# A transformer block in which the token range is worked in two halves from attention on, and a second block of tokens fetches its expert rows

## The chip, the cores and the metric

The kernel runs on one core of one Trainium2 chip. The metric is the device time of one execution in microseconds (us). A core has a matrix engine (PE, with its weight loads listed as PEld), a vector engine (DVE), a scalar engine (ACT), a general engine (POOL) and queues that issue transfers (SP above all). Sixteen DMA engines move data between HBM and the on-chip memory.

## What is computed

One layer on 512 tokens of width 2048, all in float32:

```python
h = rmsnorm(x, norm_mix_g)
proj = einsum('bsd,de->bse', h, w_in)
o_a = mla_branch(...)                  # 8 heads, chunk-causal softmax attention
o_b = dsa_branch(...)                  # 8 heads, keys chosen by a top-256 index score
merged = gate[0] * (o_a @ w_branch_a) + gate[1] * (o_b @ w_branch_b)
x = x + merged @ w_out
x = x + peer_ffn(rmsnorm(x, norm_ffn_g), ...)
return rmsnorm(x, norm_final_g)
...
# peer_ffn, for each token t: 8 heads x 16 experts of 16384 are chosen
a = gelu(einsum('thkd,td->thk', u_emb[expert], xb))
out = einsum('thk,thkd->td', softmax(top_s) * a, v_emb[expert])
```

The 512 tokens are four blocks of 128, called 0 to 3. U and V are the expert tables, 16384 rows of 2048 numbers each (134 MB each).

## The kernel before

**Precision.** Large matrix products are made of three products: each operand is split into a high part `hi` (rounded by ACT, line 77) and a rest `lo` (a subtraction of two on-chip tiles, line 78), and `mm3` (lines 101 to 104) adds hi*hi, hi*lo and lo*hi. `wload` loads 512 KB of weights, and splits them; the subtraction is DVE's unless `eng` names POOL.

**Order of the stages.** `mixing` projects the input and does attention for all four blocks. `emit` then forms the gated branches (loop over `f`, lines 151 to 166; 512 columns a product) and the output projection with the residual (lines 177 to 189; each weight load serves four blocks). `peer` normalises, asks which experts each token chooses (`wq`, then the top-16 searches of lines 684 to 699 on DVE), and evaluates them in two ways:

- Block 0 (`GB`) is fetched: `gathers` (lines 617 to 633) fetches 128 times one U row for each of the 128 tokens with an indirect DMA that POOL issues, and DVE multiplies and sums (line 623); then 128 times one V row, which DVE scales and adds to the sum (line 632). The row buffer `r` has three places.
- Blocks 1 to 3 are dense: `u_chunk` (lines 602 to 613) multiplies 128 experts at a time with 384 tokens, and `g_d`, a table in HBM with the weight of every expert for every token, made by `weights` (lines 734 to 774), switches off all that were not chosen. V is then multiplied in 16 groups of 8 chunks (lines 820 to 875), with 512 columns of V a product and three token blocks as weights.

**What sets the order.** The 54 (`NS`) first U chunks are done before V begins, along with `weights`, and wait in HBM (`s_d`); the other 74 are done group by group beside V. `tick` hands out the 256 fetches of block 0 over the V stage, each tied behind a `mark` instruction. Each engine executes its instructions in a fixed order that the planner wrote out at build time.

Of the kernel before, what the change touches and what calls it, by code (L numbers as in the profile page):

```python
# [30 lines left out]
NEXP = 16384  # L31
ND = 3
TD = ND * P
GB = 0
NS = 54
# [17 lines left out]
def emit(tc, a, out, dbg=None):  # L53
    nc = tc.nc
    with ExitStack() as top:
# [3 lines left out]
        ident = cp.tile([P, P], F32, name="ident")  # L59

        sig_d = dr.tile([KT, P, 2, S], F32, name="sig_d")
        x1_d = dr.tile([NB, P, D], F32, name="x1_d")
        s_d = dr.tile([NS, P, TD], F32, name="s_d")
        g_d = dr.tile([TD // TG, P, P * TG], F32, name="g_d")
        h2_d = dr.tile([P, D], F32, name="h2_d")

        def wload(src, eng=None):

            n = 1
            for d_ in src.shape[1:]:  # L70
                n *= d_
# [8 lines left out]

        def xraw(src):
            raw = wp.tile([P, 1024], F32, name="raw", tag="raw", bufs=4)
            nc.sync.dma_start(raw, src)
            return raw

        def rows_by_cols(pw, src, xh, xl, eng=None, head=0):

            ws = [None] * 8
            order = [(q, tb) for tb in range(NB) for q in range(head)]
            order += [(q, tb) for q in range(head, 5) for tb in range(NB)]  # L90
            order += [(q, tb) for tb in range(NB) for q in range(5, 8)]
            for q, tb in order:
                if ws[q] is None:
                    ws[q] = wload(src[q], eng)
# [37 lines left out]
        p_st, o_st, m_st, mh_st, x1_st, hg_st = [ExitStack() for _ in range(6)]  # L132
        ps = p_st.enter_context(tc.tile_pool(name="ps", bufs=2, space=PSUM))
        with ExitStack() as mix:
            oT = mixing(tc, nc, a, dbg, mix, o_st, ps, ident, sig_d, wload, mm3, rstd_of, xraw)
        if dbg:
            dbg("oT", oT)


        ohl = m_st.enter_context(tc.tile_pool(name="ohl", bufs=1))  # L140
        oh = ohl.tile([P, 16, S], F32R, name="oh")
        ol = ohl.tile([P, 16, S], F32R, name="ol")
        for k in range(16):
            nc.scalar.copy(oh[:, k, :], oT[:, k, :])
            nc.vector.tensor_sub(ol[:, k, :], oT[:, k, :], oh[:, k, :].bitcast(F32))
        o_st.close()
        mhl = mh_st.enter_context(tc.tile_pool(name="mhl", bufs=1, side="right"))
        mh = mhl.tile([P, KT, S], F32R, name="mh")
        ml = mhl.tile([P, KT, S], F32R, name="ml")
        with tc.tile_pool(name="mt", bufs=2) as tp:  # L150
            for f in range(KT):
                sg = tp.tile([P, 2, S], F32, name="sgl")
                nc.sync.dma_start(sg, sig_d[f])
                pa = []
                for br in range(2):
                    wh, wl = wload(a["wbr"][f, br])
                    pm = ps.tile([P, S], F32, name="pm", tag=("mm", "po")[br])
                    for k in range(8):
                        mm3(pm, wh[:, k * P:(k + 1) * P], wl[:, k * P:(k + 1) * P],
                            oh[:, 8 * br + k, :], ol[:, 8 * br + k, :], k == 0, k == 7)  # L160
                    pa.append(pm)
                nc.vector.tensor_mul(sg[:, 0, :], pa[0], sg[:, 0, :])
                nc.vector.tensor_mul(sg[:, 1, :], pa[1], sg[:, 1, :])
                nc.gpsimd.tensor_add(sg[:, 0, :], sg[:, 0, :], sg[:, 1, :])
                nc.scalar.copy(mh[:, f, :], sg[:, 0, :])
                nc.vector.tensor_sub(ml[:, f, :], sg[:, 0, :], mh[:, f, :].bitcast(F32))
        m_st.close()
        hgp = hg_st.enter_context(tc.tile_pool(name="hg", bufs=1))
        hg = [hgp.tile([P, KT, P], F32R, name="hgh"), hgp.tile([P, KT, P], F32R, name="hgl")]
        x1p = x1_st.enter_context(tc.tile_pool(name="x1", bufs=1))  # L170
        xg = x1p.tile([P, NB, D], F32, name="xg")
        ssq = cp.tile([P, NB, 4], F32, name="ssq")
        np_ = x1_st.enter_context(tc.tile_pool(name="n2", bufs=2))
        grow = np_.tile([P, D], F32, name="grow", bufs=1)
        nc.sync.dma_start(grow, a["gffn_row"])
        with tc.tile_pool(name="mt2", bufs=4) as tp:
            for db in range(4):
                pw = [ps.tile([P, 512], F32, name=f"pw{tb}", tag=("sc", "tr", "mm", "po")[tb]) for tb in range(NB)]
                rows_by_cols(pw, a["wo"][db], lambda tb, k: mh[:, k, tb * P:(tb + 1) * P],
                             lambda tb, k: ml[:, k, tb * P:(tb + 1) * P])  # L180
                for tb in range(NB):
                    xs = tp.tile([P, 512], F32, name="xs")
                    nc.sync.dma_start(xs, a["x"][tb * P:(tb + 1) * P, db * 512:(db + 1) * 512])
                    nc.vector.tensor_add(xs, pw[tb], xs)
                    sq = tp.tile([P, 512], F32, name="sqx", bufs=2)
                    nc.scalar.activation(sq, xs, AF.Square, accum_out=ssq[:, tb, db:db + 1])
                    (nc.vector if db == 3 else nc.gpsimd).tensor_mul(
                        xg[:, tb, db * 512:(db + 1) * 512], xs, grow[:, db * 512:(db + 1) * 512])
                    nc.scalar.dma_start(x1_d[tb, :, db * 512:(db + 1) * 512], xs)
        mh_st.close()  # L190
        if dbg:
            dbg("x1", x1_d)
        peer(tc, nc, a, dbg, out, cp, ident, p_st, x1_st, hg_st, xg, hg, np_, ps, grow, ssq, x1_d, s_d, g_d, h2_d, wload, rows_by_cols, mm3, rstd_of, turn_norm)


def mixing(tc, nc, a, dbg, mix, outer, ps, ident, sig_d, wload, mm3, rstd_of, xraw):

    mp = mix.enter_context(tc.tile_pool(name="mix", bufs=1))
    cm = mp.tile([P, 5, P], F32, name="cm")
    R_M, K_1, K_R, I_1, I_R = [cm[:, j, :] for j in range(5)]  # L200
    cmask = mp.tile([P, S], F32, name="cmask")
    ones = mp.tile([P, P], F32, name="ones")
    nc.vector.memset(ones, 1.0)
    gq = mp.tile([P, 6], F32, name="gq")
    cos0 = mp.tile([P, S], F32, name="cos0")
# [24 lines left out]
    def rope_near(dst, src, cs, half, tp):  # L230
# [7 lines left out]
        dst = sh if dst is None else dst  # L238
        nc.vector.tensor_add(dst, t1, sh)
        return dst  # L240

    def stacked(two, lo, src):

        for t in two:
# [734 lines left out]
```

## Time and profile before

| | us |
|---|---|
| median of three runs | 3678.89 (3674.55 to 3680.96) |
| profiled execution | 3671.36 |
| its span, first to last instruction | 3669.3 |

"Busy" is time in which at least one instruction of an engine runs, waits inside the instruction included. Matrix products overlap, so their cost is read from the distance between their starts. [...] MB is a million bytes.

### The profile page before, as it was taken

Reading aid. Unit: us, or ns where it says so; the run is one execution under the profiler, and the core shown is the slowest. Engines: PE = TensorE matmul, PEld = TensorE weight load, DVE = VectorE, ACT = ScalarE, POOL = GpSimd, SP = SyncE. Lnnn points to the kernel's source line nnn. Section 1 sums busy time; section 2 is a strip of 40 time slices with the busy share of each in tenths; the row PEclk is TensorE's granted clock in tenths of the full one; section 3 lists DMA queues with packets and bytes.
Section 4 is the critical chain, followed back from the end, with each engine's and each line's share of the span. In section 5 each row is a group of like instructions: output and inputs, shape, how many; then the busy total and the mean of one; then the engine's idle time right before and its main releaser. Section 6 shows DMA issues by size and latency. Waiting matters only on the chain.

```text
span 3669.3 us, 46374 instructions
## 1 busy us (share of the span) xinstructions
PE 3588.8 (98%) x17863; PEld 3151.9 (86%) x17863; DVE 2477.1 (68%) x3587; ACT 1223.0 (33%) x1621; POOL 818.2 (22%) x522
## 2 busy tenths in 40 slices
PE   8999999999999999889999999999999999999998
PEld 7878888778888789889998877889989988998997
DVE  8687322357432459999725877878777777777775
ACT  5432222245222323345433322323323322332333
POOL 3001000000101142565301222233222222222221
PEclk9999999999999999999999999999999999999999
DMA  5322333310544424445757898888788888888874
GB/s 164 105 83 92 113 120 116 114 41 27 155 149 138 138 75 135 161 148 200 257 153 237 313 316 304 316 306 325 293 309 335 291 309 323 310 299 323 318 285 169
DMA packets 259852, 767.26 MB, mean 209 GB/s; under 512 B 20528, under 2 KB 84912, under 8 KB 222128
## 3 DMA queue, kind: packets, MB, share of 16 engines
q1 hardware_dynamic: 204480, 446.43, 37.5%
q0 software_dynamic: 36864, 268.45, 18.8%
q10 hardware_dynamic: 18288, 49.42, 3.5%
q8 instruction: 140, 2.29, 0.2%
q14 instruction: 80, 0.66, 0.1%
HBM read 708.00 MB, written 53.61 MB: 208 GB/s over the span
## 4 chain that ended last, share of the span: by engine, by line
PE 90%; DVE 6%; DMA 1%; issue 1%; ACT 1%; POOL 0%; SPq 0%; DVEq 0%; ACTq 0%; POOLq 0%
PE pv L103 9%; PE pv L102 9%; PE pv L104 9%; PE pu L104 9%; PE pu L103 9%; PE pu L102 9%; PE pm L102 8%; PE pm L103 8%; PE pm L104 8%; PE pg L757 2%; PE pw L103 2%; PE pw L102 2%; PE pw L104 2%; DVE lo L78 1%; DMA s<-s_d 1%
## 5 line engine op out<-in xcount | busy, mean ns | idle before, releaser
L78 DVE TENSOR_TENSOR lo<-raw,hi 128x1024 fp32r<-128x1024 f32 (+1 forms) x700 | 888.9, 1274 | 803.3 <-issue 290.5
L77 ACT CAST hi<-raw 128x1024 fp32r<-128x1024 f32 (+1 forms) x722 | 758.9, 1052 | 1862.5 <-PE pu L103 553.0
L104 PE MATMUL pu<-h2h,lo 128*128 128x384 f32 x2048 | 698.7, 341 | 1.7 <-DVE lo L78 1.7
L102 PE MATMUL pu<-h2h,hi 128*128 128x384 f32 x2048 | 696.1, 340 | 0.5 <-ACT s L612 0.5
L103 PE MATMUL pu<-h2l,hi 128*128 128x384 f32 x2048 | 695.5, 340 | 0.0
L103 PE MATMUL pv<-lo,ch 128*128 128x512 f32 x1552 | 605.1, 390 | 12.6 <-DVE lo L78 12.6
L104 PE MATMUL pv<-hi,cl 128*128 128x512 f32 x1552 | 601.0, 390 | 0.0
L102 PE MATMUL pv<-hi,ch 128*128 128x512 f32 x1552 | 588.0, 390 | 4.5 <-ACT ch L836 3.1
L621 POOL DMA_INDIRECT r<-in_u,idx x128 | 238.5, 1863 | 767.4 <-DVE dots L623 737.8
L104 PEld LDWEIGHTS pu<-h2h,lo 128*128 128x128 f32 x2048 | 387.3, 189 | 2.9 <-DVE lo L78 2.4
L102 PEld LDWEIGHTS pu<-h2h,hi 128*128 128x128 f32 x2048 | 387.3, 189 | 1.2 <-ACT s L612 0.8
L103 PEld LDWEIGHTS pu<-h2l,hi 128*128 128x128 f32 x2048 | 387.0, 189 | 0.5
L103 PE MATMUL pm<-lT,hi 128*128 128x512 f32 (+1 forms) x912 | 356.4, 391 | 0.0
L102 PE MATMUL pm<-hT,hi 128*128 128x512 f32 (+1 forms) x912 | 356.1, 390 | 0.0
L103 PEld LDWEIGHTS pv<-lo,ch 128*128 128x128 f32 x1552 | 292.1, 188 | 74.1 <-DVE lo L78 13.9
L104 PE MATMUL pm<-hT,lo 128*128 128x512 f32 (+1 forms) x912 | 355.7, 390 | 0.0
L102 PEld LDWEIGHTS pv<-hi,ch 128*128 128x128 f32 x1552 | 292.0, 188 | 66.1 <-ACT ch L836 3.8
L104 PEld LDWEIGHTS pv<-hi,cl 128*128 128x128 f32 x1552 | 292.1, 188 | 60.7
L630 POOL DMA_INDIRECT r<-in_v,idx x128 | 205.5, 1605 | 575.1 <-DVE acc L632 554.3
L632 DVE SCALAR_TENSOR_TENSOR acc<-r,dots,acc 128x2048 f32<-128x2048 f32 x128 | 300.1, 2345 | 0.2
L623 DVE CUSTOM_DVE_ANT_0 r<-r,h2g 128x2048 f32<-128x2048 f32 x128 | 288.7, 2286 | 3.2 <-DMA r<-in_u,idx 3.2
L103 PEld LDWEIGHTS pm<-lT,hi 128*128 128x128 f32 x912 | 171.7, 188 | 39.1 <-issue 3.4
(291 smaller groups left out, 4371.1 us busy)
## 6 DMA issues: line engine op xcount, KB each, us to landing
raw<-in_ut SPq DMA_DIRECT2D x256, 512.0 KB
raw<-in_v SPq DMA_DIRECT2D x256, 512.0 KB
raw<-in_win SPq DMA_DIRECT2D x114, 512.0 KB
g_d<-gs ACTq DMA_DIRECT2D x24, 1024.0 KB
gt<-g_d SPq DMA_DIRECT2D x16, 1536.0 KB
raw<-in_wbr SPq DMA_DIRECT2D x32, 512.0 KB
raw<-in_wo SPq DMA_DIRECT2D x32, 512.0 KB
s_d<-s ACTq DMA_DIRECT2D x54, 192.0 KB
```

The lines of the kernel that those rows point to most:

```text
L77: nc.scalar.copy(hi, raw)
L78: (eng or nc.vector).tensor_sub(lo, raw, hi.bitcast(F32))
L102: nc.tensor.matmul(ps, wh, xh, start=first, stop=False)
L103: nc.tensor.matmul(ps, wh, xl, start=False, stop=False)
L104: nc.tensor.matmul(ps, wl, xh, start=False, stop=last)
L621: nc.gpsimd.indirect_dma_start(out=r, out_offset=None, in_=a["u"], in_offset=bass.IndirectOffsetOnAxis(ap=idx[:, j:j + 1], axis=0))
L623: nc.vector.tensor_tensor_reduce(out=r, in0=r, in1=h2g, scale=1.0, scalar=0.0, op0=ALU.mult, op1=ALU.add, accum_out=dots[:, j:j + 1])
L630: nc.gpsimd.indirect_dma_start(out=r, out_offset=None, in_=a["v"], in_offset=bass.IndirectOffsetOnAxis(ap=idx[:, j:j + 1], axis=0))
L632: nc.vector.scalar_tensor_tensor(accs[GB], r, dots[:, j:j + 1], accs[GB], ALU.mult, ALU.add)
L757: end[0] = nc.tensor.matmul(pg[:, j], o2[:, j, :], og[:, j, :], start=True, stop=True)
```

## The change

From attention on, everything is done for blocks 0 and 1 first and then for blocks 2 and 3.

- `attention`, `branches` and `residual` are called twice, with 256 columns a product where there were 512. Weights are loaded and split twice; keys and values of the first half are computed twice. `other()` gives every second `lo` of these stages to POOL.
- After the first half the experts of blocks 0 and 1 are asked for (`queries`). Their top-16 searches (`experts_of`) run as `side_work`, one head after each attention head of the second half.
- Block 1 fetches its U rows too. Its scores go into `g_d` in place of the softmax weights, so that its V stays dense: U has 256 dense tokens (`TU`) and V 384 (`TD`).
- `Pace` hands out 384 fetches in the order U of block 1, U of block 0, V of block 0, from the second half's `branches` on: 0.2 per us of planned time, 0.06 during the first 24 U chunks, 0.2 after them, and what is left evenly over the V stage. `weights` of block 1 first takes all fetches up to the 128th.
- `NS` is 104, and one step of `weights` is taken per chunk instead of three. `low` gives POOL one of the two `lo` of each of the first 104 chunks, and of every second one of the rest; in the V stage POOL has one `lo` of four. A second copy of V, `vd`, lies in HBM so that a load has 4 KB runs instead of 2 KB.

```diff
-GB = 0
-NS = 54
+TU = 2 * P
+NS = 104
...
+    def tick(self, mark, weight):
+        self.due += weight * self.rate
+        while self.due >= 1.0:
+            self.due -= 1.0
+            self.taken += 1
+            with self.tc.issue_after(mark.ins):
+                next(self.steps, None)
+
+    def upto(self, n):
+        while self.taken < n:
+            self.taken += 1
+            next(self.steps, None)
...
+        def other():
+
+            turn_w[0] += 1
+            return nc.gpsimd if turn_w[0] % 2 else nc.vector
...
+        def gathers():
+
+            for b in (1, 0):
+                for j in range(P):
+                    r = rp.tile([P, D], F32, name="r")
+                    nc.gpsimd.indirect_dma_start(out=r, out_offset=None, in_=a["u"],
+                                                 in_offset=bass.IndirectOffsetOnAxis(ap=idx[b][:, j:j + 1], axis=0))
+                    nc.vector.tensor_tensor_reduce(out=r, in0=r, in1=h2g[b], scale=1.0, scalar=0.0,
+                                                   op0=ALU.mult, op1=ALU.add, accum_out=dots[b][:, j:j + 1])
...
+        RATE = (0.2, 0.06, 0.2)
...
+        def low(c):
+
+            return (nc.gpsimd if c < NS or c % 2 else None, None)
...
+        fetch = Pace(tc, gathers(), RATE[0])
...
+        for i in range(2):
+            blocks = (2 * i, 2 * i + 1)
...
+                attention(i, oT, lambda mark, weight: None, side_work)
...
+                branches(i, mh, ml, oh, ol, tick, side_work)
...
+                residual(i, mh, ml, xg, grow, tick)
...
+                    for half in range(2):
+                        pw = queries(0, half, parts, ps)
...
+                side_work = experts_of(qT, aq)
...
+                    if tb == 1:
+                        fetch.upto(P)
+                        key, g = key1, dots[1]
...
+                def routes():
+                    for tb in (2, 3, 1):
+                        yield from weights(tb - 1, tb)
...
-            for c in range(NS - NF):
-                s = u_chunk(c, (nc.gpsimd if c < 6 else None, None))
-                nc.scalar.dma_start(s_d[c], s)
-                for _ in range(3):
-                    next(todo, None)
+                for c in range(NS - NF):
+                    s, mark = u_chunk(c, low(c))
                     nc.scalar.dma_start(s_d[c], s)
+                    fetch.rate = RATE[1] if c < 24 else RATE[2]
+                    tick(mark, 5.7)
+                    steps += 103.0 / (NS - NF)
+                    while steps >= 1.0:
+                        steps -= 1.0
+                        next(todo, None)
...
+            fetch.rate = (3 * P - fetch.taken) / ((P - NS) * 5.7 + P * 8.2 - 30.0)
...
+                            s3 = s.rearrange("p (b t) -> p b t", t=TG)
+                            nc.vector.tensor_mul(s3, s3, gt[:, P // TG:, ci, :])
+                            parts3 = [(gt[:, :P // TG, ci, :], slice(0, P)), (s3, slice(P, TD))]
+                            for src, w in parts3:
+                                h3, l3 = [t[:, w].rearrange("p (b t) -> p b t", t=TG) for t in (hi, lo)]
+                                nc.scalar.copy(h3, src)
+                                mark = nc.vector.tensor_sub(l3, src, h3.bitcast(F32))
...
+                                ws[q] = wload(a["vd"][c // 2, db], nc.gpsimd if q == 1 else None)
```

## Rows read from the trace of the kernel before

**Rows 1.** Busy time by engine, from the page.

```profile
PE 3588.8 (98%) x17863; PEld 3151.9 (86%) x17863; DVE 2477.1 (68%) x3587; ACT 1223.0 (33%) x1621; POOL 818.2 (22%) x522
```

**Rows 2.** Stretches: us; busy PE, PEld, DVE, ACT, POOL; clock, DMA share, GB/s.

```profile
709.00:900.00 191.00, 185.88 (x1146) 157.71 (x1145) 117.09 (x408) 93.59 (x230) 10.32 (x8) 1.00 0.13 38
900.00:1074.00 174.00, 173.97 (x766) 143.80 (x767) 76.57 (x93) 49.77 (x61) 20.05 (x15) 1.00 0.46 142
1074.00:1254.00 180.00, 180.00 (x775) 144.97 (x773) 56.29 (x68) 45.43 (x65) 19.91 (x15) 1.00 0.43 139
...
1375.00:1967.00 592.00, 564.57 (x3417) 556.45 (x3415) 468.42 (x881) 245.19 (x285) 219.82 (x158) 0.98 0.53 174
1967.00:2380.00 413.00, 399.01 (x1745) 329.33 (x1746) 331.78 (x385) 125.20 (x150) 102.87 (x56) 0.99 0.89 312
2380.00:3593.00 1213.00, 1213.00 (x6133) 1111.80 (x6132) 945.41 (x822) 373.68 (x439) 337.07 (x197) 1.00 0.85 309
```

**Rows 3.** The stretch of the normalisation and of `wq`.

```profile
1254.00:1375.00 121.00, 115.02 (x562) 96.24 (x561) 65.84 (x316) 39.19 (x56) 43.90 (x27) 0.97 0.31 98
```

**Rows 4.** Timeline of PE, U products: start, us, line, tiles, shape.

```profile
1900.11 0.34 PE L102 MATMUL pu<-h2h,hi 128*128 128x384 f32 x1
...
1906.87 0.34 PE L102 MATMUL pu<-h2h,hi 128*128 128x384 f32 x1
```

**Rows 5.** Timeline of PE, products of 272 columns at the start.

```profile
35.82 0.29 PE L104 MATMUL pd<-hi,lT 128*128 128x272 f32 x1
...
37.19 0.29 PE L103 MATMUL pd<-lo,hT 128*128 128x272 f32 x1
```

**Rows 6.** DVE's top-16 searches, one of the five operations of either width.

```profile
L688 DVE FIND_INDEX8 inds<-vals,wk 128x8 uint32<-128x128 f32 x64 | 18.3, 288 | 0.0
...
L698 DVE FIND_INDEX8 posn<-tops,cand 128x8 uint32<-128x256 f32 x32 | 13.5, 423 | 0.0
```

**Rows 7.** DVE's groups in the V stage (1967 to 3593): count, busy us, mean ns.

```profile
L78 DVE TENSOR_TENSOR lo<-raw,hi 128x1024 fp32r<-128x1024 f32 x388 | 471.9, 1222 | 201.9 <-issue 90.8 <-PE pv L103 59.1 <-ACT hi L77 28.8
L632 DVE SCALAR_TENSOR_TENSOR acc<-r,dots,acc 128x2048 f32<-128x2048 f32 x127 | 297.8, 2345 | 0.2
L623 DVE CUSTOM_DVE_ANT_0 r<-r,h2g 128x2048 f32<-128x2048 f32 x128 | 288.7, 2286 | 3.2 <-DMA r<-in_u,idx 3.2
L868 DVE TENSOR_TENSOR acc<-pv,acc 128x512 f32<-128x512 f32 x180 | 122.3, 687 | 43.7 <-PE pv L104 43.7
L833 DVE TENSOR_TENSOR s<-s,gt 128x384 f32<-128x384 f32 x127 | 69.9, 557 | 55.6 <-DMA s<-s_d 45.8 <-DMA gt<-g_d 6.0 <-ACT s L612 3.0
```

**Rows 8.** DVE's groups while the routes are made (1437 to 1805).

```profile
L749 DVE TENSOR_TENSOR og<-iota,kt 128x512 f32<-128x512 f32 x96 | 112.8, 1175 | 0.0
L78 DVE TENSOR_TENSOR lo<-raw,hi 128x1024 fp32r<-128x1024 f32 x59 | 101.3, 1719 | 0.0
L750 DVE TENSOR_TENSOR o<-iota,kt 128x512 f32<-128x512 f32 x96 | 72.7, 758 | 0.0
L719 DVE TENSOR_TENSOR eq<-sf,iota 128x512 f32<-128x512 f32 x32 | 31.1, 986 | 0.1
```

**Rows 9.** That stretch (1437 to 1805) as a whole.

```profile
1437.00:1805.00 368.00, 343.18 (x2151) 337.60 (x2151) 358.63 (x526) 173.32 (x195) 197.98 (x140) 0.96 0.51 173
```

**Rows 10.** POOL's groups over the whole execution.

```profile
L621 POOL DMA_INDIRECT r<-in_u,idx x128 | 238.5, 1863 | 767.4 <-DVE dots L623 737.8 <-issue 29.0 <-DVE idx L780 0.4
...
L751 POOL TENSOR_TENSOR og<-og,kt 128x512 f32<-128x512 f32 x96 | 136.3, 1419 | 94.6 <-DVE og L749 94.6
L78 POOL TENSOR_TENSOR lo<-raw,hi 128x1024 fp32r<-128x1024 f32 x22 | 52.9, 2419 | 91.6 <-PE pq L104 50.3 <-PE pw L103 38.5 <-issue 2.8
```

**Rows 11.** Timeline of POOL: an `og`.

```profile
1700.76 1.42 POOL L751 TENSOR_TENSOR og<-og,kt 128x512 f32<-128x512 f32 x1 [0.63 <-DVE og L749]
```

**Rows 12.** Timeline of DVE: a `lo` beside it.

```profile
1701.20 2.06 DVE L78 TENSOR_TENSOR lo<-raw,hi 128x1024 fp32r<-128x1024 f32 x1
```

**Rows 13.** A short stretch of high DMA load, columns as in rows 2.

```profile
2000.00:2020.00 20.00, 20.00 (x90) 16.57 (x89) 14.97 (x16) 4.91 (x5) 4.21 (x3) 1.00 1.00 375
```

More of the change, by code (lines that the diff above doesn't have):

```diff
@@ L142, in emit @@
[L142 to L166, printed above, removed]
@@ L176, in emit @@
[L176 to L189, printed above, removed]
@@ new lines, in rope_near @@
+        def rope_near(dst, src, cs, half, tp):
+            n = src.shape[1]
+            sh = tp.tile([P, S], F32, name="rt2", tag="rt2")[:, :n]
+            nc.vector.stream_shuffle(sh, src, [i ^ half for i in range(32)])
+            t1 = tp.tile([P, S], F32, name="rt1", tag="rt1")[:, :n]
+            nc.gpsimd.tensor_mul(t1, src, cs[0])
+            nc.vector.tensor_mul(sh, sh, cs[1])
+            if dst is None:
+                nc.vector.tensor_add(sh, t1, sh)
+            else:
+                for d_, w in dst:
+                    nc.vector.tensor_add(d_, t1[:, w], sh[:, w])
+            return sh
@@ new lines, in stacked, with mm_stacked @@
+        def stacked(two, lo, src):
+            for t in two:
+                nc.scalar.copy(t, src)
+            nc.vector.tensor_sub(lo, src, two[0].bitcast(F32))
+            nc.sync.dma_start(two[0][64:, :].bitcast(F32), lo[:64, :].bitcast(F32))
+            nc.sync.dma_start(two[1][:64, :].bitcast(F32), lo[64:, :].bitcast(F32))
+        def mm_stacked(ps_, two, hh, cols, kh, kl, n, first, last):
+            rows = slice(64 * hh, 64 * hh + 64)
+            nc.tensor.matmul(ps_, two[hh][:, cols], kh[:, :n], start=first, stop=False)
+            nc.tensor.matmul(ps_, two[hh][rows, cols], kl[rows, :n], start=False, stop=last)
@@ new lines, in branches @@
+        def branches(i, mh, ml, oh, ol, tick, side_work):
+            with tc.tile_pool(name=f"mt{i}", bufs=2) as tp:
+                for f in range(KT):
+                    sg = tp.tile([P, 2, HB], F32, name="sgl")
+                    nc.sync.dma_start(sg, sig_d[i, f])
+                    pa = []
+                    for br in range(2):
+                        wh, wl = wload(a["wbr"][f, br], other())
+                        pm = ps.tile([P, S], F32, name="pm", tag=("mm", "po")[br])[:, :HB]
+                        for k in range(8):
+                            mm3(pm, wh[:, k * P:(k + 1) * P], wl[:, k * P:(k + 1) * P],
+                                oh[:, 8 * br + k, :], ol[:, 8 * br + k, :], k == 0, k == 7)
+                        pa.append(pm)
+                    nc.vector.tensor_mul(sg[:, 0, :], pa[0], sg[:, 0, :])
+                    nc.vector.tensor_mul(sg[:, 1, :], pa[1], sg[:, 1, :])
+                    nc.gpsimd.tensor_add(sg[:, 0, :], sg[:, 0, :], sg[:, 1, :])
+                    tick(halves([mh[:, f, :], ml[:, f, :]], sg[:, 0, :]), 5.7)
+                    next(side_work, None)
@@ new lines, in experts_of @@
+        def experts_of(qT, gp):
+            for tb in (1, 0):
+                got = picks(gp, "")
+                for half in range(2):
+                    yield from best(half, qT[tb, half], gp, ps, keys_of(half, gp), *got)
+                key = decode(tb, gp, *got, gsel[tb])
+                expert_numbers(gp, key, idx[tb])
+                if tb == 1:
+                    nc.vector.tensor_copy(key1, key)
+                known.append(tb)
+                yield
+        known = []
+        fetch = Pace(tc, gathers(), RATE[0])
```

1273 lines of the change are left out of this document (646 added, 627 removed).

## The prediction

> **What bounds the kernel now.** I read the busy times first: PE is busy for 3588.8 us of a span of 3669.3, so matrix work sets the end [rows 1]. Then the stretches [rows 2, 3]. PE is full in nearly all of them, and the reader is to see the exceptions: 592 us in which the first U chunks and the routes are made, with 27 us of PE idle, and the 413 us after it, with 14. In the first the cause is DVE: between 1437 and 1805 it is busy for 358.63 of 368 us [rows 9]. In the V stage (1967 to the end) DVE is at 78 to 80% and DMA at 0.85 to 0.89 of its engines' time. Last the groups of DVE and POOL [rows 6 to 8, 10] and two places of the timeline [rows 4, 5, 11, 12] for prices.
>
> **What U gives back.** Starts of U products are (1906.87 - 1900.11) / 39 = 0.173 us apart at 384 columns [rows 4], those of 272 columns (37.19 - 35.82) / 11 = 0.1245 [rows 5], those of 512 columns 174 / 768 = 0.2266 [the branches, rows 2]. The slope is 0.43 ns a column, so 256 columns cost 0.118. Weight loads stay hidden at 272, so I see no floor before 256. U has 128 chunks of 48 products: 6144 x (0.173 - 0.118) = 338 us less, and a chunk is 5.66 us instead of 8.3.
>
> **What the halves cost.** The branches become 1536 products of 0.118, 181 us for 174. The output projection and `wq` keep their products (180 us, and most of 121 [rows 2, 3]). Attention was 191 us with PE at 186. Keys and values of the first half made twice add 24 products of 512 columns and 48 of 256 (11 us). The first half has short rows, and its second eight heads are small chains of DVE and ACT: I take 80 us, by the 117 us of DVE now, of which a good third falls to it. The second half would be 128 us by PE, but the searches of blocks 0 and 1 now sit between its heads. A search of one head is 10 operations of about 0.288 and 5 of about 0.423 [rows 6], 5 us, so 16 heads are 80 us of DVE, with some 25 for two decodes, on top of about 70 of its own: 170 us (ends: 128 if PE hides it, 190). Attention thus goes from 191 to 250. The loads and `lo` of the doubled weights are covered in the first half: a load serves 2.8 us of PE there, against 1.2 (DVE) or 2.4 us (POOL) for every second one.
>
> **What DVE and POOL take on.** 128 fetches more are 128 x 2.29 us of DVE [rows 7], and each moves 1.05 MB (128 rows of 8 KB). POOL gets 104 + 12 `lo` of U, 64 of V and half of those of the second branches and projection, at 2.42 us [rows 10] where DVE needs 1.22 [rows 7].
>
> The two engines are not independent here. A POOL `og` ran from 1700.76 to 1702.18 [rows 11]; a DVE `lo`, 1.22 us alone, began at 1701.20 and took 2.06 [rows 12]. It ended 1.08 us after POOL, as if it had begun only then. In the groups, `lo` is 1.72 us beside POOL for 1.22 without it, and `og` 1.18 for the same-sized `o`'s 0.76 [rows 7, 8]. I therefore count operations of DVE that read two on-chip tiles and POOL's arithmetic one after the other. No row shows a fetch multiply beside POOL arithmetic; bounds are not held at all and held in full, and I take full, since like `lo` it reads two tiles on the chip.
>
> [...]
>
> **The stages from the second half on**, in us:
>
> Branches and projection of blocks 2 and 3: PE 181; DVE's two-tile work 32 `lo` at 1.08, 36 fetches at 2.15 and small ones 4, 116; POOL 32 `lo` and small ones, 95. Together 211; I take 210 (ends 181, 230).
>
> U stage (from the second `wq`, 104 chunks): PE has 104 x 5.66 = 589, half of `wq` 46 and some 110 for the products of routes and searches (the 565 us of PE in the 592 us stretch less 54 old chunks [rows 2]): 745. By the pace 36 fetches are out before it, 8 follow in 24 chunks, 87 in the next 76, and the call for the 128th adds 35, so 129 in all. DVE's two-tile work is 104 x 1.08 + 192 tables x 0.62 + 129 x 2.15 + 10 = 518. POOL's arithmetic is 104 + 16 `lo` at 2.42, 96 `og` at 1.42 and 16 small ones, 450. One after the other that is 968. The same count for 1437 to 1805 gives 203 + 198 = 401 against 368, so it overstates by a twelfth: 888. I take 920 (ends 745, 995). What is late next is the U `lo`, so PE waits; and block 1's routes, which wait for its 128th fetch and hold the last four chunks and the V stage. DMA would need 236 MB in the 76 chunks, at 375 GB/s [rows 13] 629 us, and the stage 46 + 152 + 629 + 23 = 850: below 920.
>
> V stage: 4608 x 0.2266 + 24 x 5.66 + 15 for the end = 1195. DVE: 228 `lo` 279, 219 fetches 514, coefficients about 1.1 us a chunk 143 (by the 0.557 of one of today's two operations), 192 sums 132: 1068, and part of POOL's 76 x 2.42 = 184 comes in between. DMA moves 438 MB, 1168 us at 375 GB/s. All three are near 1195, and in the 413 us without U work beside V PE lost 14 with lighter ones [rows 2]; that state lasts 13 groups instead of 6. I add 40: 1235 (ends 1205, 1290). The 4 KB runs of V are worth nothing on the path unless DMA binds.
>
> **The sum**: 709 (unchanged) + 250 + 181 (first branches and projection) + 60 (normalisation, `wq`) + 210 + 13 + 920 + 1235 = 3578, against 3669. The gain of 338 is eaten by attention (59), branches and projection (37), and waits in the U and V stages. The execution shown is 2 us longer than its span, and the median 7.5 us above that: 3590.
>
> **The rivals.**
>
> *The fetch multiply is not held by POOL, or the two dovetail.* Then DMA paces the U stage at 850, and the second branches fall to 185: 3480 to 3500, down to 3430 if the stage's DVE gaps close too. For it: no row shows this operation blocked. Against it: `lo` is.
>
> *PE alone sets the pace.* 709 + 203 + 181 + 60 + 181 + 13 + 745 + 1195 = 3287, about 3300. Against it: the 888 to 968 us that DVE and POOL need one after the other in the U stage would have to fit into 745.
>
> *POOL's queue delays the weights (slower).* POOL works in a fixed order. Today each of its fetches of U rows sits 767 / 128 = 6 us at the head of that order until DVE frees a row buffer [rows 10], which hurts nobody, since nothing that PE needs is behind it. After the change 180 `lo` of U and V weights stand there, and behind each of them PE. Whenever DVE runs later than planned, a `lo` that could start waits for a buffer. With 89 us in hand, an average loss of 0.5 us of PE for each of the 180 makes the change slower; at 1 us the time is 3770. For it: DVE near its limit is just where it is late. Against it: three `lo` buffers run ahead by some 5 us.
>
> *The change doesn't do what it says:* the shorter U product could meet a floor of the weight load. The even 0.1245 at 272 columns speaks against it.
>
> **How the numbers follow.** Within 0.2% of the time before counts as no change; a measurement here can't tell less. Mine, 3530 to 3660: 0.38. DMA's pace, 3430 to 3530: 0.22. PE alone: 0.04. No change: 0.06. POOL's queue: 0.30. So faster 0.64, same 0.06, slower 0.30. The range reaches from 3440, short of PE alone, to 3750, most of POOL's queue; my own case has 3530 to 3660.
>
> **What would show it.** U products 0.118 apart. DVE `lo` and fetch multiplies well above 1.22 and 2.29 us beside POOL's work in the U stage, with DVE over 95% busy and PE at some 80%. Second attention about 170 us with DVE full. If instead fetch multiplies stay at 2.29, the first rival holds; if PE waits for POOL's `lo` while POOL sits before a fetch, the third. I am wrong in the mechanism if the U stage is under 800 us, or if PE's idle time lies mainly in the V stage.

## The result and the profile after

The changed kernel takes 3826.68 us (median; 3822.48 to 3830.9) against 3677.27 of the kernel before in the same session: a ratio of 1.0406, 95% interval 1.0388 to 1.0424. It is slower by 150 us where I had forecast 87 us faster, and above the top of my range. Its profiled execution took 3830.9 us, its span is 3829.1.

Busy time by engine, from the page of the kernel after (beside [rows 1]):

```profile
PE 3433.8 (90%) x18855; PEld 2974.1 (78%) x18855; DVE 2878.8 (75%) x3900; ACT 1316.0 (34%) x1916; POOL 1735.2 (45%) x938
```

PE does 155 us less and stands idle for 395 us instead of 81. DVE has 402 us more, POOL 917. Where the idle time lies, the stretches show, cut at the stages of the prediction (columns as in [rows 2], the clock as a share of full speed): attention, branches with projection, and normalisation with `wq` of the first half; attention, branches with projection, and normalisation of the second; the U stage in two parts; the V stage.

```profile
708.00:800.00 92.00, 82.28 (x544) 72.51 (x542) 52.72 (x221) 50.32 (x147) 21.02 (x14) 0.94 0.24 72
800.00:991.00 191.00, 180.93 (x1156) 162.70 (x1156) 78.72 (x107) 82.79 (x108) 101.46 (x55) 0.98 0.70 229
991.00:1045.00 54.00, 53.06 (x259) 44.52 (x260) 7.62 (x17) 26.18 (x29) 33.58 (x14) 0.96 0.41 129
1045.00:1225.00 180.00, 149.54 (x871) 124.42 (x869) 145.94 (x632) 70.14 (x159) 41.88 (x38) 0.96 0.16 50
1225.00:1490.00 265.00, 201.73 (x1153) 176.38 (x1152) 228.12 (x209) 82.50 (x109) 194.70 (x100) 0.90 0.85 304
1490.00:1505.00 15.00, 10.60 (x64) 10.24 (x64) 12.00 (x18) 4.69 (x8) 2.49 (x4) 0.73 0.72 255
1505.00:2330.00 825.00, 630.83 (x4305) 594.61 (x4305) 779.33 (x914) 279.11 (x338) 591.56 (x321) 0.87 0.76 276
2330.00:2567.00 237.00, 217.37 (x1702) 214.62 (x1703) 105.63 (x81) 90.13 (x118) 120.03 (x54) 0.94 0.83 293
2567.00:3829.00 1262.00, 1215.03 (x5764) 1015.21 (x5763) 1092.27 (x1140) 407.54 (x609) 575.05 (x301) 0.98 0.91 340
```

Beside the prediction: 92 for 80, 191 for 181, 54 for 60, 180 for 170, 265 for 210, 15 for 13, 1062 for 920 and 1262 for 1235. Of the 251 us that the sum was short, 142 lie in the U stage and 55 in the second branches. In the U stage up to 2330 the reader is to see DVE at 779 of 825 us while PE gets 68 of the 104 chunks done (the gelus in that stretch); the other 36 follow in 237 us, with DVE at less than half.

What PE waits for in that stretch (us in total, times, longest):

```profile
PE pu L147 <- DVE lo L114: 111.5, 44, 10.5
PE pg L869 <- POOL og L863: 32.6, 16, 5.8
PE pu L147 <- POOL lo L114: 23.0, 18, 2.6
```

It is DVE's `lo` that is late, by up to 10.5 us, and much less POOL's. The DVE groups of the U stage (1505 to 2567; columns as in [rows 6]), and POOL's `lo`:

```profile
L269 DVE CUSTOM_DVE_ANT_0 r<-r,h2g 128x2048 f32<-128x2048 f32 x128 | 374.2, 2943 | 35.4 <-DMA r<-in_u,idx 35.3
L114 DVE TENSOR_TENSOR lo<-raw,hi 128x1024 fp32r<-128x1024 f32 x105 | 192.4, 1841 | 124.5 <-PE pu L147 89.1 <-ACT hi L113 25.3 <-issue 10.1
L861 DVE TENSOR_TENSOR og<-iota,kt 128x512 f32<-128x512 f32 x96 | 130.7, 1362 | 6.6 <-PE pg L869 6.5
L862 DVE TENSOR_TENSOR o<-iota,kt 128x512 f32<-128x512 f32 x96 | 105.0, 1094 | 0.0
L246 DVE TENSOR_REDUCE key<-eq 128x32 f32<-128x512 f32 x16 | 10.8, 673 | 0.0
L209 DVE FIND_INDEX8 inds<-vals,wk 128x8 uint32<-128x128 f32 x32 | 8.8, 280 | 0.0
```

```profile
L114 POOL TENSOR_TENSOR lo<-raw,hi 128x1024 fp32r<-128x1024 f32 x118 | 320.4, 2721 | 129.0 <-PE pu L147 74.4 <-ACT hi L113 42.7 <-issue 8.6
```

The fetch multiply takes 2.94 us for 2.29 and `lo` 1.84 for 1.22 [rows 7]; the searches (`FIND_INDEX8`, 0.280 for 0.288 [rows 6]) take what they took. Single instructions show the cause, first on DVE, then on POOL (timelines; start and duration in us):

```profile
1741.42 3.81 DVE L269 CUSTOM_DVE_ANT_0 r<-r,h2g 128x2048 f32<-128x2048 f32 x1
...
1751.29 5.00 DVE L114 TENSOR_TENSOR lo<-raw,hi 128x1024 fp32r<-128x1024 f32 x1
```

```profile
1741.78 1.30 POOL L245 TENSOR_TENSOR eq<-eq,inf 128x512 f32<-128x512 f32 x1
...
1751.63 1.27 POOL L245 TENSOR_TENSOR eq<-eq,inf 128x512 f32<-128x512 f32 x1
1752.85 2.35 POOL L114 TENSOR_TENSOR lo<-raw,hi 128x1024 fp32r<-128x1024 f32 x1
```

The multiply lasted 1.53 us longer than the 2.28 it takes alone (e8), with 1.30 us of POOL arithmetic inside it. The `lo` at 1751.29 ended 1.09 us after the second of two POOL operations, as if it had begun only then. In these rows the multiply, too, is held.

U products came as cheap as forecast where nothing was late: 52 of them began between 2479.8 and 2485.9, 0.12 us apart.

### The profile page after: what moved, and what is told of

It reads as the page before. It is cut to its first block, busy times and chain, and to the rows that moved or that the text cites. A ratio compares the mean times of both kernels' runs of the same rounds, so it can differ in the third digit from the quotient of the medians.

```text
span 3829.1 us, 50476 instructions
## 1 busy us (share of the span) xinstructions
PE 3433.8 (90%) x18855; PEld 2974.1 (78%) x18855; DVE 2878.8 (75%) x3900; ACT 1316.0 (34%) x1916; POOL 1735.2 (45%) x938
## 4 chain that ended last, share of the span: by engine, by line
PE 35%; DVE 13%; issue 6%; DMA 4%; POOL 3%; ACT 1%; ACTq 0%; SPq 0%; DVEq 0%; POOLq 0%
PE pv L146 8%; PE pv L147 8%; PE pv L145 8%; PE pu L147 3%; DVE lo L114 3%; PE pu L146 3%; PE pu L145 3%; DVE r L269 3%; DMA raw<-in_ut 2%; POOL lo L114 2%; DVE o L862 2%; DVE og L861 2%; DMA raw<-in_vd 1%; ACT hi L113 1%; PE pg L869 1%
## 5 line engine op out<-in xcount | busy, mean ns | idle before, releaser
L113 ACT CAST hi<-raw 128x1024 fp32r<-128x1024 f32 (+1 forms) x812 | 838.2, 1048 | 1124.6 <-PE pm L146 437.5
L114 DVE TENSOR_TENSOR lo<-raw,hi 128x1024 fp32r<-128x1024 f32 (+1 forms) x526 | 736.8, 1411 | 600.8 <-PE pm L147 200.0
L114 POOL TENSOR_TENSOR lo<-raw,hi 128x1024 fp32r<-128x1024 f32 x286 | 762.6, 2670 | 747.4 <-PE pm L147 350.7
L147 PE MATMUL pu<-h2h,lo 128*128 128x256 f32 x2048 | 617.9, 304 | 172.3 <-DVE lo L114 134.3
L269 DVE CUSTOM_DVE_ANT_0 r<-r,h2g 128x2048 f32<-128x2048 f32 x256 | 700.7, 2752 | 38.7 <-DMA r<-in_u,idx 38.5
L145 PE MATMUL pu<-h2h,hi 128*128 128x256 f32 x2048 | 612.7, 299 | 13.0 <-ACT hi L113 12.2
L267 POOL DMA_INDIRECT r<-in_u,idx x256 | 413.7, 1616 | 443.7 <-DVE dots L269 347.7
L146 PE MATMUL pu<-h2l,hi 128*128 128x256 f32 x2048 | 607.4, 297 | 0.0
L145 PE MATMUL pv<-hi,ch 128*128 128x512 f32 x1536 | 548.9, 392 | 2.4 <-ACT ch L946 1.8
L282 DVE SCALAR_TENSOR_TENSOR hacc<-r,dots,hacc 128x2048 f32<-128x2048 f32 x128 | 320.8, 2506 | 0.8 <-DMA r<-in_v,idx 0.3
```

What stands on the lines that cost most here:

```text
L113: nc.scalar.copy(hi, raw)
L114: (eng or nc.vector).tensor_sub(lo, raw, hi.bitcast(F32))
L145: nc.tensor.matmul(ps, wh, xh, start=first, stop=False)
L146: nc.tensor.matmul(ps, wh, xl, start=False, stop=False)
L147: nc.tensor.matmul(ps, wl, xh, start=False, stop=last)
L267: nc.gpsimd.indirect_dma_start(out=r, out_offset=None, in_=a["u"], in_offset=bass.IndirectOffsetOnAxis(ap=idx[b][:, j:j + 1], axis=0))
```

## The experiments

All times are medians, each with the ratio to the kernel before run beside it (3679.7 to 3681.3 us) and its 95% interval. Theory A, the hold with the sum of both engines' work, was set against DVE's load alone (B), POOL's order (C), crowded work (D, J), DMA traffic (E), something else that holds the stage (G), ACT's load (H), and the price of the halves (F).

**e1, weight rests on DVE.**

```diff
-            return (nc.gpsimd if c < NS or c % 2 else None, None)
+            return (None, None)
-            return nc.gpsimd if turn_w[0] % 2 else nc.vector
+            return nc.vector
-                         lambda tb, k: parts[tb][1][:, k, :], blocks, lambda: nc.gpsimd, 0 if half else 2)
+                         lambda tb, k: parts[tb][1][:, k, :], blocks, lambda: nc.vector, 0 if half else 2)
```

> The changed kernel with every second-half, U and wq weight rest (lo) on DVE; POOL keeps its other arithmetic and its one lo of four in the V stage. Theory A, the hold: a POOL lo shuts DVE's two-tile work out for its 2.4 us and saves DVE only 1.22, so some 150 of them taken away from the stretches where DVE is full shorten these by 90 to 140 us: 3690 to 3740. Theory B, DVE's own load is the bound and POOL relieves it: 115 lo more in 1225 to 2330 at 1.22 us lengthen it by 140: 3900 to 3970. Theory C, PE waits for POOL's lo in POOL's order: PE loses only the 61 us it waits for POOL's lo, 3770 to 3800.

Measured 3754.47, 1.0208 (1.0189 to 1.0227): 72 us faster than the changed kernel. B falls: DVE's work grows and the time shrinks. From 1225 to the first V product (1342 us of the changed kernel, 1273 here) DVE takes 286 rests instead of 136, and its busy time falls from 1125 to 1088. C's number is just missed as well; A's range, 3690 to 3740, lay 15 us too low.

**e2, routes tied to their chunks.**

```diff
                         steps -= 1.0
-                        next(todo, None)
+                        with tc.issue_after(mark.ins):
+                            next(todo, None)
```

> The changed kernel with each step of weights tied behind the gelu of the chunk it was written beside, so that the planner cannot draw the routes forward. Theory D, crowding: the routes end at 2330 with only 68 of 104 chunks done and DVE is 45% busy in the 237 us left, so the spread fills those 130 us of DVE: 60 to 120 us less, 3710 to 3770. Theory A alone (the sum of DVE and POOL work is what counts, wherever it stands): within 20 us of 3827. Rival: the last four chunks wait longer for the routes and the V stage starts later, 3850 to 3900.

Measured 3828.66, 1.0405 (1.0384 to 1.0425): no change, as A says. The routes now run to 2525, and V begins at 2564 as before (2567). D falls for this kernel.

**e3, hardly any multiply for block 1.**

```diff
-                    nc.vector.tensor_tensor_reduce(out=r, in0=r, in1=h2g[b], scale=1.0, scalar=0.0,
+                    n = D if b == 0 else 64
+                    nc.vector.tensor_tensor_reduce(out=r[:, :n], in0=r[:, :n], in1=h2g[b][:, :n], scale=1.0, scalar=0.0,
```

> The changed kernel with the multiply of block 1's fetched rows over 64 of 2048 columns only; the fetches themselves are all there (what is left out: 97% of 128 multiplies). Theory A or B, DVE is what the fetches cost: some 128 x 2.8 = 355 us of DVE are gone, the second branches and projection fall from 265 to about 190 and the U stage from 1062 to 830 to 900: 3560 to 3640. Theory E, the fetches cost by their DMA traffic (0.76 to 0.9 of the engines' time there): both stretches stay within 30 us, 3790 to 3830.

Measured 3737.66, 1.0156 (1.0134 to 1.0178). Both numbers miss. DVE is rid of some 300 us and only 89 come back, though DVE is now at 669 of 1011 us in the U stage (1475 to 2486). PE's waits there:

```profile
PE pu L147 <- POOL lo L114: 56.3, 30, 4.6
PE pu L147 <- DVE lo L114: 43.7, 21, 6.2
PE pu L145 <- ACT hi L113: 41.6, 18, 7.7
```

It waits for three engines in turn, none of them full. So the multiply is not the whole price of the fetches; POOL's `lo`, of which 118 are left, is late more often than DVE's (30 times against 21).

**e4, the halves alone**, first attempt (the core of its edit; block 1's columns are a copy of block 2's).

```diff
-TU = 2 * P
+TU = 3 * P
...
-            for b in (1, 0):
+            for b in (0,):
...
-        RATE = (0.2, 0.06, 0.2)
+        RATE = (0.0, 0.0, 0.0)
...
-                        fetch.upto(P)
-                        key, g = key1, dots[1]
+                        key, g = key1, gsel[1]
```

> The changed kernel with block 1 dense in U again (384 columns a product; its third block of columns is a copy of block 2's, so block 1's U values are those of block 2), no fetch of block 1, and block 0's 256 fetches spread over the V stage only. This is the cost of the halves by itself: PE has as much as before plus the doubled keys and branches. Theory F, the halves cost what they measured (attention 272 for 191, branches and projection 191 plus about 190 for 354, norm and wq the same): before plus 90 to 110, 3770 to 3790, so block 1's fetches as made now cost 40 to 60 us more instead of giving 338. Rival: with U dense, the held POOL lo keep costing in the U stage as well, 3830 or more. Rival: the halves cost next to nothing without fetches, 3680 to 3720.

Measured 3860.87, 1.0496 (1.0473 to 1.0519). It doesn't answer: the last sum of the dense blocks began at 3758.5, and then block 0's fetches ran on, the last at 3841.

**e5, e1 and e3 together.**

> Both edits of the first and the third experiment: weight rests on DVE, and the multiply of block 1's rows over 64 of 2048 columns (97% of 128 multiplies left out). Theory A, the sum of DVE's work and POOL's arithmetic sets the U stage: rests 254, tables 145, short and long multiplies 150, small ones 12, one-tile work 120, POOL 170, together 850 for the 1010 of e1, and the second branches 50 less: 3540 to 3610. Theory G, something else holds the stage near 1010 (late transfers or the fixed orders): both edits give hardly more than one, 3680 to 3740.

Measured 3669.8, 0.9974 (0.9961 to 0.9987), between the two ranges. The edits add up (72 and 89, together 157), but the U stage is 944 us (1460 to 2404; 992 in e1), not 850: PE is full only from some 2200 on, when the routes are over.

**e6, no traffic of block 1's fetches.**

```diff
-                    nc.gpsimd.indirect_dma_start(out=r, out_offset=None, in_=a["u"],
+                    if b == 0 or j == 0:
+                        nc.gpsimd.indirect_dma_start(out=r, out_offset=None, in_=a["u"],
...
+                    if b and j == 0:
+                        rz = rp.tile([P, D], F32, name="rz", bufs=1)
+                        nc.vector.tensor_copy(rz, r)
-                    nc.vector.tensor_tensor_reduce(out=r, in0=r, in1=h2g[b], scale=1.0, scalar=0.0,
+                    nc.vector.tensor_tensor_reduce(out=r, in0=rz if b else r, in1=h2g[b], scale=1.0, scalar=0.0,
```

> The changed kernel without the transfers of 127 of block 1's 128 fetches; their multiplies run in full over one row that stays on the chip (what is left out: 133 MB of traffic and 127 issues on POOL). Theory A: DVE and POOL arithmetic have the same work, so 3780 to 3830. Theory E, the traffic: the second branches and the U stage lose the 133 MB (355 us of all engines at 375 GB/s) and PE's weights come earlier, 3620 to 3720.

Measured 3783.19, 1.027 (1.0246 to 1.0295): A's range, and E falls. 133 MB less give 44 us. Traffic is not what lengthens the multiply either: those of block 1 (1225 to 2518) take as long as in the changed kernel, though DMA is down to 0.61 of its engines' time in the U stage (1563 to 2518) from 0.78:

```profile
L273 DVE CUSTOM_DVE_ANT_0 r<-rz,h2g 128x2048 f32<-128x2048 f32 x128 | 374.7, 2957 | 0.0
```

**e7, `og` times `g` on ACT** (on top of e1).

```diff
-                        nc.gpsimd.tensor_mul(og, og, kt[:, 2, t:t + 4, None].to_broadcast([P, 4, P]))
+                        for j in range(4):
+                            nc.scalar.activation(og[:, j, :], og[:, j, :], AF.Copy, scale=kt[:, 2, t + j:t + j + 1])
```

> The first experiment (rests on DVE) with the 96 products og*g of the routes on ACT, as 384 copies with a scale, instead of on POOL. Theory A: POOL's 136 us of arithmetic leave the U stage and what they held of the tables and multiplies comes back, 3754 less 90 to 140: 3610 to 3665, below the kernel before. Rival H: ACT gets 384 x 0.3 = 115 us in front of its hi copies and gelus, PE waits for these, 3740 to 3800.

Measured 3659.79, 0.9944 (0.9922 to 0.9965). A's range, and the first complete version faster than the kernel before: 96 POOL operations of 1.3 us were worth 95 us. C may have a part in this, since PE also waited for the product `og` itself; in e1 (1225 to 2498) and here (1225 to 2400):

```profile
PE pg L869 <- POOL og L863: 58.5, 40, 5.5
...
PE pg L870 <- ACT og L864: 18.7, 18, 2.8
```

What DVE gets back is enough for the whole gain: its busy time in the U stage falls from 852 to 763 us, as the stage falls from 992 to 902.

**e8, no POOL arithmetic after the projection** (on top of e7; `cand`, `eq` and the product with `grow` go from `nc.gpsimd` to `nc.vector` in the same way, the one with `gfin` at the very end stays).

```diff
-                                ws[q] = wload(a["vd"][c // 2, db], nc.gpsimd if q == 1 else None)
+                                ws[q] = wload(a["vd"][c // 2, db], None)
-                    nc.gpsimd.tensor_add(sg[:, 0, :], sg[:, 0, :], sg[:, 1, :])
+                    nc.vector.tensor_add(sg[:, 0, :], sg[:, 0, :], sg[:, 1, :])
...
```

> The seventh experiment with the rest of POOL's arithmetic after the projection on DVE too: eq and cand of the searches, the sums of the branches, and the one rest of four in the V stage. POOL then issues fetches and little else. Theory A: the 74 rests of the V stage cost POOL 180 us of hold and DVE 90, so V shortens by 20 to 40 and the second branches by 20: 40 to 60 below e7. Theory B: DVE, with 1084 of 1260 us busy in the V stage, takes 90 more and becomes late there: 10 to 60 above e7.

Measured 3640.69, 0.9887 (0.9865 to 0.9909): 19 below e7, on A's side but short of its 40. Its DVE groups in the U stage (1502 to 2405):

```profile
L269 DVE CUSTOM_DVE_ANT_0 r<-r,h2g 128x2048 f32<-128x2048 f32 x126 | 287.2, 2280 | 3.7 <-DMA r<-in_u,idx 3.6
L114 DVE TENSOR_TENSOR lo<-raw,hi 128x1024 fp32r<-128x1024 f32 x223 | 270.1, 1218 | 128.1 <-PE pu L147 94.0 <-ACT hi L113 33.2 <-issue 0.8
L861 DVE TENSOR_TENSOR og<-iota,kt 128x512 f32<-128x512 f32 x96 | 65.8, 686 | 5.1 <-PE pg L870 4.8
L862 DVE TENSOR_TENSOR o<-iota,kt 128x512 f32<-128x512 f32 x96 | 65.7, 684 | 0.0
```

Multiply and `lo` are back at their times alone [rows 7], the tables (`og` and `o`) at 0.69, beside more DMA traffic (0.90 of the engines' time for 0.78). Against these, the changed kernel's U stage held DVE for 128 x 0.66 + 105 x 0.62 + 96 x (0.68 + 0.41) + 16 x 0.53 (`eq`) = 263 us. U stage and V stage as a whole:

```profile
1502.00:2405.00 903.00, 792.36 (x6040) 758.84 (x6041) 764.97 (x1147) 481.80 (x844) 149.52 (x127) 0.97 0.90 327
2405.00:3638.00 1233.00, 1201.46 (x5763) 1002.17 (x5761) 1089.39 (x1215) 407.96 (x609) 371.48 (x225) 1.00 0.93 348
```

**e9, e8 with e2's tie.**

> The eighth experiment with the steps of weights tied behind their chunks, as in the second. Theory D, crowding, now that POOL holds nothing: in e8 DVE is full up to 2200 and busy for 94 of the 211 us from there to the end of the U stage, so a spread can use some 100 us of it: 3560 to 3610. Rival: what delays PE is the order in which each engine takes its work and not the sum, as in e2: 3620 to 3660.

Measured 3629.6, 0.9868 (0.9847 to 0.9889): the rival's range; D falls again.

**e10, the halves alone, second attempt** (e4 with `RATE = (0.0, 0.0, 0.1)`).

> The fourth experiment with 0.1 fetches of block 0 per us from the 25th U chunk on, since in e4 block 0's last fetches ended 100 us after the other work. Theory F: the halves alone with a dense block 1 end where e4's matrix work did, 3760 to 3790, so that the halves cost 80 to 110 us. Rival: the fetches still end last, 3820 or more.

Measured 3846.7, 1.0453 (1.0435 to 1.047). That is in the rival's range, but not for its reason: the fetches end at 3792 and the matrix work at 3833. Again no answer, for a part of the fetches ran in the second branches, which took 256 us (202 without, in e15). The fetches of U rows up to 2500:

```profile
L267 POOL DMA_INDIRECT r<-in_u,idx x46: 937/1760/3032, 1285.9 to 1533.1; - x46
```

They are written behind the U chunks 24 to 99 and ran before the first. In the U stage the mark is ACT's gelu, and here it held back neither POOL's fetches nor DVE's multiplies. In the changed kernel, too, 34 multiplies ran from 1490 to 1700 beside 14 chunks, for which some 5 were written. With a mark on DVE (e13) it is 8 beside 19 chunks.

**e11, 44 rests more on POOL in the kernel before.**

```diff
-                s = u_chunk(c, (nc.gpsimd if c < 6 else None, None))
+                s = u_chunk(c, (nc.gpsimd, None))
```

> The kernel before with the first of the two rests of each of the first 50 U chunks on POOL (6 before). Theory A, the hold: while the routes are made DVE is full, and each of some 36 rests there costs 2.4 us of hold for 1.22 saved, so the kernel gets 20 to 45 us slower: 3700 to 3725. Theory B, relief: DVE is rid of 54 us where it is the bound, and PE's 27 idle us there shrink: 3650 to 3670.

Measured 3702.73, 1.0053 (1.0036 to 1.007): slower, as A says and B denies. In 1437 to 1805 PE's busy time falls from 343 [rows 9] to 327 us; some 10 of these 16 us are longer waits for POOL's own results (`og` 12.2 to 16.0, `lo` none to 6.7).

**e12, the kernel before with e8's edits.**

> The kernel before with what e8 did to the changed one: og*g of the routes on ACT, all rests, eq, cand, the branches' sums and the weighted residual on DVE. Theory A: the stretch in which DVE is full eases and most of the 41 us that PE idles in the U and early V stages come back: 3635 to 3665. Then the change, with POOL out of the way in both, is worth little: e8 is within 25 us of it. Rival: PE is at 98% and nothing moves, 3670 to 3685.

Measured 3631.45, 0.9864 (0.9847 to 0.988), slightly better than A's range. The stretch of [rows 9]:

```profile
1437.00:1805.00 368.00, 368.00 (x2378) 367.62 (x2376) 315.06 (x689) 276.94 (x574) 11.46 (x3) 1.00 0.57 189
```

PE is full in it, with 2378 products for 2151, though DVE and ACT have taken over POOL's work.

**e13, the pace kept, in the changed kernel.** Here `wload` notes its subtraction in `last[0]`:

```diff
-                    return s, nc.scalar.activation(s, pu, AF.Gelu)
+                    nc.scalar.activation(s, pu, AF.Gelu)
+                    return s, last[0]
```

> The changed kernel with one thing altered: in the U stage the mark behind which a fetch is tied is the rest of the chunk's second weight load, on DVE, and no longer the gelu on ACT. The trace shows that the written pace isn't kept there: 34 multiplies in 1490 to 1700, in 14 chunks, where 0.06 per us stands for 5. Theory J, the fetches come too early and crowd the routes: with the pace kept the U stage shortens by 40 to 90 us, 3740 to 3790. Theory A: the sum of DVE's and POOL's work is the same, 3800 to 3850.

Measured 3839.73, 1.0442 (1.0416 to 1.0467): A's range. Keeping the pace alone helps nothing.

**e14, e9 with e13's mark.**

> The ninth experiment with fetches and routes tied behind the rest on DVE, as in e13. Theory J: DVE is busy for 800 of the 935 us of the U stage, full up to 2200 and half idle after; with the pace kept its work spreads and the stage takes 850 to 890, 3550 to 3590. Rival: 35 fetches are now due at once at the call for block 1's 128th, at chunk 67, and what they push back holds the last chunks: 3630 to 3680.

Measured 3627.51, 0.9862 (0.984 to 0.9884): by the median no more than e9, and the rival just missed. Four executions took 3626.41 to 3629.78 and the profiled one 3603.16, so its stages aren't used.

**e15, the halves alone, third attempt** (e4's edit with 0.1 fetches per us from chunk 24, e8's and e13's).

> The halves alone (block 1 dense in U by a copy of block 2's columns, 384 columns a product, no fetch of block 1) with POOL's arithmetic out of the way as in e8 and the fetches of block 0 tied as in e13, to be set against the kernel before with the same mend (e12, 3631). Theory F: the doubled keys and branches and the searches between the heads cost what e4's stages show, 70 to 100 us: 3700 to 3730. Rival: most of that price was POOL's hold too, 3640 to 3670.

Measured 3747.06, 1.0182 (1.0157 to 1.0207): 116 us above e12. Its second branches, its U stage and its V stage:

```profile
1225.00:1427.00 202.00, 190.88 (x1188) 172.84 (x1188) 147.00 (x267) 84.50 (x111) 4.03 (x3) 0.96 0.72 228
...
1434.00:2450.00 1016.00, 1012.55 (x6041) 1001.52 (x6041) 587.68 (x971) 492.95 (x837) 41.58 (x43) 1.00 0.63 210
2450.00:3748.00 1298.00, 1267.19 (x5760) 1068.81 (x5760) 1093.69 (x1083) 399.99 (x489) 360.07 (x219) 0.99 0.88 331
```

Its attentions take 91 and 180 us for 191 of [rows 2] and its branches with projection 191 and 202 for 354: 80 and 39 more, which is the whole difference in span to e12 (3747.8 - 3628.8 = 119).

**e16, even pace** (on top of e14).

```diff
-        RATE = (0.2, 0.06, 0.2)
+        RATE = (0.2, 0.2, 0.2)
-                    steps += 103.0 / (NS - NF)
+                    steps += 69.0 / 80 if c < 80 else 34.0 / 20
```

> The fourteenth experiment with 0.2 fetches per us all through the U stage, and the routes of blocks 2 and 3 over the first 80 chunks, those of block 1 over the last 20, so that nothing is due in a burst. Theory J: DVE's 800 us lie evenly, 3540 to 3580, below e14. Rival, PE waits by the order within each chunk and not by any burst: within 15 us of e14 and e9, 3615 to 3645.

Measured 3603.83, 0.9796 (0.9771 to 0.9821): the fastest of all, though short of J's range. It is faster than e9 by 26 us, and than e14 by 24; but one of e14's five executions was as short as these, so what the even pace adds to e14 is not settled. The same stages as for e15:

```profile
1225.00:1483.00 258.00, 202.52 (x1188) 178.74 (x1188) 220.37 (x333) 84.73 (x111) 57.96 (x38) 0.90 0.86 318
...
1490.00:2322.00 832.00, 769.93 (x6042) 745.98 (x6042) 737.36 (x1119) 484.76 (x840) 147.33 (x115) 0.98 0.92 338
2322.00:3600.00 1278.00, 1208.18 (x5763) 1001.00 (x5761) 1126.15 (x1253) 410.06 (x616) 350.26 (x240) 0.98 0.93 349
```

With POOL out of the way, block 1's fetches cost 56 us in the second branches and give 184 in the U stage and 20 in V.

**The parts of the change, from these runs:** halves +116 (e12 to e15); block 1's U rows fetched -106 as planned (e15 to e8) and -143 with an even pace (to e16); POOL's arithmetic +186 in the changed kernel (e8 to 3827) and +50 in the one before (e12 to 3681). Between the profiles of e8 and of the changed kernel these 186 lie in the U stage (1062 us against 903) and the V stage (1262 against 1233); the second branches are no shorter in e8 (269 against 265).

## Why the prediction was wrong

**The mechanism held.** DVE's two-tile operations take longer beside POOL's arithmetic (`lo` 1.84 us for 1.22, the tables 1.36 and 1.09 for 0.69 and 0.68); the fetch multiply is held as I took it (2.94 for 2.28); DVE's `lo` is what comes late (PE waits 111.5 us for it); PE is not the bound of the U stage (busy for 848 of 1062 us) and is near it in the V stage (1215 of 1262). Up to 2330 DVE is at 94% and PE at 76%, near the 95 and 80 that were to show it. e1, e7, e8, e11 and e12 move POOL's work in either direction, in both kernels, and the time follows each time. PE's direct waits for POOL's results (33 us for `og` and 58 for `lo` in the changed kernel) may have a part in this; no run takes them away by themselves.

**The step that failed is the sum of the U stage**: "One after the other that is 968. The same count for 1437 to 1805 gives 203 + 198 = 401 against 368, so it overstates by a twelfth: 888. I take 920." The stage took 1062. By DVE's time these are 622 us of its own work (885 us busy, less the 263 of hold worked out at e8), 263 of hold, and 177 in which DVE is idle. My 920 were 518 of DVE's own work, 402 that POOL's arithmetic adds, and no idle time. All three terms are wrong:

- DVE's own work was 104 short. I counted only its two-tile operations. The top-16 searches of blocks 2 and 3 run in this stage as well, 16 heads at the 5 us that I had counted for blocks 0 and 1 in attention, and decodes and accumulator reads: by their groups some 115 us (records of neighbours overlap a little, those at 1741.42 and 1745.17 by 0.06 us, so the sum of groups is more than the busy time). The searches take no more time beside POOL's arithmetic (0.280 us for 0.288 [rows 6]), but they take DVE's.
- What POOL adds was 139 too high: not all of its arithmetic fell on two-tile operations of DVE.
- DVE's idle time I put at nothing, without a reason. Of its 177 us, 131 lie in the last 237, in which the routes are over and PE, busy for 217 of them, works off 36 chunks. The longest idle time by group, 124.5 us, is before `lo`, 89.1 of it for PE.

The twelfth was taken off for the overlap in a stretch of 368 us; it scaled a sum whose terms were wrong. Without it and with the searches the count is 968 + 115 = 1083, within 2% of the stage, but that is luck: what it has too much for POOL and what it lacks in idle time cancel. For 1437 to 1805 the same count, with some 70 us of searches, decodes and sums, gives 470 for 368.

That the uneven order by itself is the loss is refuted by e2 and e13: with the routes spread DVE is as idle (861 of 1059 us busy in e2). It is idle for 138 us of e8's 903 and for 95 of e16's 832 as well. What makes DVE and PE wait for each other there, beyond the hold, stays open. An even pace was tried only with POOL's arithmetic out of the way (e16).

**Second branches and projection**, 265 for 210. I had put down 116 us of DVE. It was busy for 228: I left out the 16 `ml` (31 us), the last decode (`eq` and its sums, 20 us) and the branches' and projection's own operations (`sgl`, `xs` and `ol`, 24 us). With POOL's arithmetic on DVE the stretch is no shorter (269 in e8); without fetches it is 202 (e15). So the fetches are worth 56 to 67 us here (to e16 and e8). Not all of that is the multiply, which takes 34 x 2.28 = 78 us of DVE: without it the stretch falls only from 265 to 241 (e3), with `lo` on DVE from 265 to 220 (e1 to e5). The rest goes with the fetches themselves.

**Attention**, 272 for 250, and the halves alone +116 (e12 to e15). My 96 (59 and 37) are not the same thing, since 29 of them stood for fetches and POOL's work in the second branches; by PE alone I had 67. The second attention took 180 for 170 with DVE at 146 of 180, not full.

**The V stage**, 1262 for 1235, is a term that was a little small: 25 us of it (1258 in e7 to 1233 in e8) go with POOL's `lo`.

**The paces** were read from the code as written: "8 follow in 24 chunks". The trace shows 34 in the first 14. It did not matter by itself (e13).

**The rivals.** The first (multiply not held) is refuted by 2.94 against 2.28 us. The second (PE alone) would have had 745 us for the U stage, which took 1062. The fourth (a floor of the weight load) falls, since U products did come 0.12 apart. The third had the right sign and the wrong cause: PE waits for POOL's `lo` for 58 us in the whole execution, not for 180. What I had given 0.30 by that mechanism came by mine, with a sum that was 251 us short; a gain of 89 us on a sum of that kind deserved less trust.

**What stays open.** PE's mean granted clock was 0.87 in 1505 to 2330, where it was busy for 631 of 825 us, 0.98 in e16's U stage (770 of 832) and 1.00 in e15's (1013 of 1016). A U product has 472.80 / 3288 = 0.144 us of busy time in that stretch of the changed kernel, for 0.128 in e16 (639.93 / 4991). Over the whole U stage that is 50 us more of PE's busy time (690 for 640). I had no term for it, and no run separates it from the waits. Nor is it settled what holds e3's U stage at 1011 us.

## What to carry to other kernels

Before work is given to POOL, count for every DVE operation beside it whether it reads two on-chip tiles: here such operations got longer beside POOL's arithmetic (`lo` 1.84 us for 1.22; 493 us of that arithmetic in this U stage cost DVE 263), while the searches did not (0.280 for 0.288). A subtraction of 1.22 us that takes 2.4 on POOL was a loss in both kernels where DVE was near its limit (e1, e11). For a stage that an engine nearly fills, sum all its groups, line by line from the trace, the small ones included; don't scale the sum down by one favourable stretch, and take it for a floor: in every version here DVE was idle for at least 95 us of the U stage. Undo a suspect by itself in both kernels: here that gave 1.4% without the change, and with it the change itself is worth nothing as planned (3641 against 3631 us) and 0.8% with an even pace (3604; the kernel before was not tuned in the same way).

## What was not expected of the hardware

- POOL's fetch issues (`DMA_INDIRECT`) don't hold DVE as its arithmetic does: in e8's U stage POOL has little else to do than issue 126 fetches, and DVE's `lo`, tables and multiplies average 1.22, 0.69 and 2.28 us, their times alone. A single case of it (DVE, then POOL):

```profile
2006.41 1.22 DVE L114 TENSOR_TENSOR lo<-raw,hi 128x1024 fp32r<-128x1024 f32 x1
...
2006.77 1.68 POOL L267 DMA_INDIRECT r<-in_u,idx  x1 [4.61 <-DVE dots L269]
```

- Not only operations that read two tiles are held. In the changed kernel a shift of integers that reads one took 2.44 us, for 0.21 of the same line at 1229.02, and ended 0.08 after a `lo` of POOL:

```profile
1711.09 2.44 DVE L236 TENSOR_SCALAR sub<-posn 128x128 int32<-128x128 int32 x1
...
1711.05 2.40 POOL L114 TENSOR_TENSOR lo<-raw,hi 128x1024 fp32r<-128x1024 f32 x1 [2.74 <-ACT s L834]
```

- The hold reaches back over an instruction that the profile lists as begun: the multiply at 1741.42 and the `lo` at 1751.29 began 0.36 and 0.34 us before POOL's operations and took 1.53 and 3.78 us longer than alone all the same.
- POOL is held as well: its `lo` takes 2.33 us at its shortest and 2.72 on average in the U stage, and the one at 1735.91 took 4.45, beside a multiply of DVE from 1735.04 to 1738.10.
